# Banks, order of products and the square of a, in a Strassen projection with a gated recurrence

## Chip, cores and metric

The kernel runs on one core of one Trainium2 chip. The metric is the device time of one execution in microseconds. Its engines are named as the profile names them: PE (TensorE) multiplies, DVE (VectorE), ACT (ScalarE) and POOL (GpSimd) work on vectors, SP (SyncE) issues the DMAs. Each works through its own list of instructions in order and waits at the first one whose inputs or target are not free.

## The reference

One layer over 1024 positions of width 2048, all in float32: an RMSNorm, one projection to 6144 columns (queries, keys, values and gate of eight attention heads; input and gate of eight recurrent blocks), the two halves, one output projection, the residual and a last RMSNorm. Cut to what the change touches:

```python
h = rms_norm(x, norm_gain[l])
proj = h @ w_in[l]                       # 1024 x 2048 @ 2048 x 6144
...
r = sigmoid(xb @ w_a + b_a)              # after a causal convolution of width 4
i = sigmoid(xb @ w_x + b_x)
log_a = -8.0 * r * softplus(-lru_lambda)
a = exp(log_a)
mult = sqrt(-expm1(2.0 * log_a))
h[t] = a[t] * h[t - 1] + mult[t] * (i[t] * x[t])
```

The kernel computes `expm1(2 log_a)` as `(a*a + 1) * tanh(log_a)`, so it needs the square of `a`.

## The kernel before

**Products.** The projection is done by blocks of two by two with seven products in place of eight (Strassen, in Winograd's form). A *pair* is two units of 128 output columns over one half of the 2048 inputs; there are 24 pairs for each half of the inputs, 48 in all. For a pair, products 0 to 6 are each twelve matmuls of 128x128 by 128x512 (L677): four blocks of the inputs, and for each the three terms of a float32 split into a high and a low part. A product collects in one PSUM bank; the bank of each is in `BANKS`: al, de, be, al, ga, be, ga for products 0 to 6. Products 3, 5 and 6 add to what the bank holds.

**What reads the banks.** `post` is called behind each product. Behind product 0, ACT copies al (a1, L546). Behind 1, DVE forms result 11 from de and a1. Behind 3, ACT copies al (u2, L552), and DVE forms be + u2 (u3). Behind 4, DVE forms result 22 from ga and u3; behind 5, result 21 from be and u2; behind 6, result 12 from ga and u2. All DVE additions go through the helper `tt`, so they stand at L193 in the profile; the splits into a high part (a cast on ACT, L189) and a low part (DVE or POOL, L190) go through `split`.

**Three segments.** Segment one forms partial results of the eight recurrent pairs over one half of the inputs, segment two all 24 pairs over the other half, segment three the sixteen attention pairs over the first half again. The first two pairs of each segment, and the last two of segments one and two, run side by side in two sets of four banks (pp0 to pp3, and pq0 to pq3). The pairs between them run one behind the other in `chained`, in the banks pp0 to pp3 alone: four pairs in segment one, twenty in segment two, fourteen in segment three. Before the change a link of that chain is 3, 4, 0', 5, 1', 6, 2', where the mark means the next pair.

**Work around it.** What follows a pair is written as generators that a counter of slots drives: one slot passes with every quarter of a product. `recurrent` (segment two) does the convolution, two gates (four groups of three matmuls into pq0 and pq1, sigmoids at L751), the tanh (L760) and the exponential (L762) of the logarithm of a, the square on POOL, (square + 1) x tanh on DVE (L770), its root on ACT (L774), the scan (L781) and the SiLU of the gate (L697, L699), whose product with the scan is made by POOL and split. `rope` and `values` (segment three) rotate q and k and transpose v (on PE, into pq0), and store them by DMA; `square` and `second_operands` (segment one) add up squares of x on ACT and POOL. pq2 and pq3 hold nothing while a chain runs. Weights are loaded and split three products ahead.

A scheduler of the language decides where an instruction stands in the list of its engine, so the lists are not the order of the code; they are fixed when the program is built. 89 buffers of 128x512 are given out in the order in which they come free, so a new use of a buffer can wait for a DMA that still reads the old content.

Of the kernel before, what the change touches and what calls it, by code (L numbers as in the profile page):

```python
# [13 lines left out]
F32 = mybir.dt.float32  # L14
# [3 lines left out]
AF = mybir.ActivationFunctionType  # L18
ALU = mybir.AluOpType
AX = mybir.AxisListType  # L20

P = 128
# [5 lines left out]
NR = 8  # L28
# [25 lines left out]
BANKS = ("al", "de", "be", "al", "ga", "be", "ga")  # L54
# [51 lines left out]
class Pair:  # L106
# [3 lines left out]
    def __init__(self, k, us, done=None, key=None):  # L110
        self.k = k
        self.us = us
        self.done = done
        self.key = key
        self.s = 0
        self.x = {}
        self.w = {}
        self.c = {}
        self.p = {}


class Trunk:
# [86 lines left out]
    def consts2(self):  # L209
# [44 lines left out]
        self.nsp = cst.tile([P, NR], F32, name="nsp")  # L254
        nc.vector.tensor_scalar_mul(self.nsp, t[4], -8.0)


# [280 lines left out]
    def partial(self, pr, name):  # L538
        p = pr.p[name] = self.alloc()
        self.load(p.f, self.part[pr.key, name])  # L540

    def post(self, pr, pi):
        nc, b = self.nc, self.bank[pr.s]
        if pi == 0:
# [20 lines left out]
    def chained(self, pairs):  # L565


        q = [(pairs[0], pi) for pi in range(3)]
        for n, p in enumerate(pairs):
            q += [(p, 3), (p, 4)]  # L570
            for pi in (5, 6):
                if p is not pairs[-1]:
                    q.append((pairs[n + 1], pi - 5))
                q.append((p, pi))
            if p is not pairs[-1]:
                q.append((pairs[n + 1], 2))
        return q

    def projection(self):
# [65 lines left out]
        for i, (p, pi) in enumerate(q):  # L645
# [24 lines left out]
            self.dual = dual  # L670
            acc = self.bank[p.s][BANKS[pi]]
            hi, lo = p.w.pop(pi)
# [30 lines left out]
    def recurrent(self, n, c4):  # L703
# [51 lines left out]
        self.rel(gw)  # L755
        sp = self.nsp[:, n:n + 1]
        th = [self.alloc(), self.alloc()]
# [3 lines left out]
        for l in range(2):  # L761
            nc.scalar.activation(a[l].f, gates[l, 0].f, AF.Exp, scale=sp)  # L762
            self.tt(gates[l, 1].f, gates[l, 1].f, cs[l].f, ALU.mult, nc.gpsimd)
            self.rel(cs[l])
            yield 1
        for l in range(2):
            r = gates[l, 0]
            self.tt(r.f, a[l].f, a[l].f, ALU.mult, nc.gpsimd)
            yield 3
            nc.vector.scalar_tensor_tensor(out=r.f, in0=r.f, scalar=1.0, in1=th[l].f,  # L770
                                           op0=ALU.add, op1=ALU.mult)
            yield 1
# [481 lines left out]
```

## Time and profile before

| | |
|---|---|
| median of 3 runs (range) | 1716.01 us (1712.44 to 1718.68) |
| the profiled execution | 1710.78 us, its span 1709.0 us |
| PE busy, DVE busy | 1561.2 us, 1278.1 us |
| ACT busy, POOL busy | 816.4 us, 615.7 us |
| granted PE clock, mean over the span | 0.972 |
| projection, then attention and output | 0 to 1102 us, 1102 to 1709 us |

The busy time of PE is an average over stages with different limits, and its matmuls overlap; what a stage loses is read from the count of its matmuls against the price of one where nothing waits, and from the waits of PE in that stage.

### The profile page before, as it was taken

Reading aid. Unit: us, or ns where it says so; the run is one execution under the profiler, and the core shown is the slowest. Engines: PE = TensorE matmul, PEld = TensorE weight load, DVE = VectorE, ACT = ScalarE, POOL = GpSimd, SP = SyncE. Lnnn points to the kernel's source line nnn. Section 1 sums busy time; section 2 is a strip of 40 time slices with the busy share of each in tenths; the row PEclk is TensorE's granted clock in tenths of the full one; section 3 lists DMA queues with packets and bytes.
Section 4 is the critical chain, followed back from the end, with each engine's and each line's share of the span. In section 5 each row is a group of like instructions: output and inputs, shape, how many; then the busy total and the mean of one; then the engine's idle time right before and its main releaser. Section 6 shows DMA issues by size and latency. Waiting matters only on the chain. (4 is left out here: it accounts for less than half of the span.)

```text
span 1709.0 us, 22289 instructions
## 1 busy us (share of the span) xinstructions
PE 1561.2 (91%) x7140; PEld 1265.1 (74%) x7140; DVE 1278.1 (75%) x2120; ACT 816.4 (48%) x1462; POOL 615.7 (36%) x486
## 2 busy tenths in 40 slices
PE   6977998998999899998998998889999999989997
PEld 4765876787777777877777777767777777868786
DVE  8856759777987889889999988857777777761412
ACT  6443633645456355653323333335665555663432
POOL 3474421424334234451222222324222322357370
PEclk9998999999999999999999999999999999999999
DMA  6665732433424332575665555877577655474642
GB/s 253 223 219 182 240 119 82 130 95 110 131 79 135 120 120 96 196 237 181 205 198 185 183 181 167 298 287 272 177 228 246 209 164 165 147 249 134 223 153 99
DMA packets 168277, 304.18 MB, mean 178 GB/s; under 512 B 19040, under 2 KB 21216, under 8 KB 168160
## 3 DMA queue, kind: packets, MB, share of 16 engines
q1 hardware_dynamic: 168160, 302.76, 53.3%
q8 instruction: 56, 0.92, 0.2%
q14 instruction: 61, 0.50, 0.1%
HBM read 206.22 MB, written 96.47 MB: 177 GB/s over the span
## 5 line engine op out<-in xcount | busy, mean ns | idle before, releaser
L677 PE MATMUL pp<-b,b 128*128 128x512 f32 x3612 | 881.8, 402 | 96.8 <-ACT b L552 49.5
L677 PEld LDWEIGHTS pp<-b,b 128*128 128x128 f32 x3612 | 696.9, 194 | 263.7 <-ACT b L552 57.5
L190 POOL TENSOR_TENSOR b<-b,b 128x512 fp32r<-128x512 f32 x288 | 429.4, 1504 | 779.8 <-ACT b L189 458.1
L189 ACT CAST b<-b 128x512 fp32r<-128x512 f32 x592 | 353.3, 619 | 526.7 <-DVE b L193 202.1
L190 DVE TENSOR_TENSOR b<-b,b 128x512 fp32r<-128x512 f32 x304 | 234.2, 785 | 74.9 <-ACT b L189 52.5
L193 DVE TENSOR_TENSOR b<-b,b 128x512 f32<-128x512 f32 x340 | 269.7, 809 | 18.0 <-DMA b<-w_in 6.3
L1099 PE MATMUL pq<-b,b 128*128 128x512 f32 x512 | 203.3, 397 | 3.6 <-DVE b L190 3.6
L1098 PE MATMUL pq<-b,b 128*128 128x512 f32 x512 | 203.6, 398 | 1.6 <-POOL b L190 1.6
L1097 PE MATMUL pq<-b,b 128*128 128x512 f32 x512 | 203.0, 397 | 0.0
L193 DVE TENSOR_TENSOR b<-pp,b 128x512 f32<-128x512 f32 x215 | 146.1, 680 | 39.3 <-ACT b L552 22.0
L193 DVE TENSOR_TENSOR b<-pq,b 128x512 f32<-128x512 f32 x89 | 61.0, 686 | 108.4 <-PE pq L1099 102.0
L900 ACT ACTIVATE wide<-sw,mx 128x256 f32<-128x256 f32 (+7 forms) x128 | 93.9, 739 | 61.7 <-DVE mx L896 60.4
L193 POOL TENSOR_TENSOR b<-b,b 128x512 f32<-128x512 f32 (+1 forms) x56 | 82.1, 1469 | 106.1 <-DVE b L699 38.3
L1099 PEld LDWEIGHTS pq<-b,b 128*128 128x128 f32 x512 | 96.7, 189 | 21.4 <-DVE b L190 5.4
L193 DVE TENSOR_TENSOR b<-b,wide 128x512 f32<-128x512 f32 x120 | 104.5, 884 | 9.7 <-ACT wide L1167 9.1
L893 DVE CUSTOM_DVE_ANT_0 sw<-sw,mask 128x256 f32<-128x256 f32 (+7 forms) x128 | 96.7, 762 | 17.9 <-PE sw L889 16.4
L1098 PEld LDWEIGHTS pq<-b,b 128*128 128x128 f32 x512 | 96.8, 189 | 17.5 <-POOL b L190 2.0
L1097 PEld LDWEIGHTS pq<-b,b 128*128 128x128 f32 x512 | 96.8, 189 | 15.9
L677 PE MATMUL pq<-b,b 128*128 128x512 f32 x420 | 104.6, 395 | 2.3 <-POOL b L190 1.0
L677 PEld LDWEIGHTS pq<-b,b 128*128 128x128 f32 x420 | 80.1, 191 | 20.3 <-POOL b L190 1.4
L1024 ACT CAST b<-pq 128x512 fp32r<-128x512 f32 (+1 forms) x80 | 43.5, 544 | 76.7 <-PE pq L1015 73.7
L888 PE MATMUL sw<-b,b 128*128 128x512 f32 (+2 forms) x192 | 70.9, 372 | 9.0 <-ACT wide L900 8.7
(149 smaller groups left out, 1574.6 us busy)
## 6 DMA issues: line engine op xcount, KB each, us to landing
b<-w_in SPq DMA_DIRECT2D x192, 256.0 KB, 2.9
b<-w_out SPq DMA_DIRECT2D x128, 256.0 KB, 4.3
pt<-b SPq DMA_DIRECT2D x96, 256.0 KB, 2.7
b<-pt SPq DMA_DIRECT2D x96, 256.0 KB, 2.9
b<-fs SPq DMA_DIRECT2D x96, 256.0 KB, 4.5
b<-xt SPq DMA_DIRECT2D x72, 256.0 KB, 3.9
fs<-b SPq DMA_DIRECT2D x64, 256.0 KB, 2.4
b<-yd SPq DMA_DIRECT2D x32, 256.0 KB, 4.6
```

The costliest lines, as they stand in the source:

```text
L189: self.nc.scalar.copy(hi.r, x)
L190: (eng or self.nc.vector).tensor_tensor(out=lo.r, in0=x, in1=hi.f, op=ALU.subtract)
L193: (eng or self.nc.vector).tensor_tensor(out=out, in0=a, in1=b, op=op)
L677: nc.tensor.matmul(acc, lhsT=a.r[:, s], rhs=b.r, start=FIRST[pi] and qq == 0 and j == 0, stop=qq == 3 and j == 2, skip_group_check=True)
L888: nc.tensor.matmul(o, lhsT=q[m].r[:, qs], rhs=kk, start=True, stop=False)
L893: nc.vector.tensor_tensor_reduce(out=s, in0=s, in1=self.mask[:, 896 - off:896 - off + cols], scale=1.0, scalar=NEG, op0=ALU.add, op1=ALU.m ...
L900: nc.scalar.activation(p[:, :cols], self.swide[m][:, :cols], AF.Exp, scale=QK ** -0.5, bias=mx[:, m:m + 1], accum_out=sm[:, m:m + 1])
L1024: nc.scalar.copy(wh.r[:, first:], self.tr[:, first:])
L1097: nc.tensor.matmul(acc, lhsT=mh.r[:, s], rhs=wh.r, start=kt == 0, stop=False)
L1098: nc.tensor.matmul(acc, lhsT=mh.r[:, s], rhs=wl.r, start=False, stop=False)
L1099: nc.tensor.matmul(acc, lhsT=ml.r[:, s], rhs=wh.r, start=False, stop=kt == 7)
```

## The change

Three edits. In a chain every second pair (`odd`) has banks of its own for al and be: pq2 and pq3. A link of the chain becomes 3, 4, 0', 1', 5, 6, 2'. And the square of a is no longer a product on POOL but a second exponential on ACT, with twice the scale (`nsp2`), written over the gate; with the product, three slots for each half fall away.

```diff
--- before.py
+++ after.py
@@ -117,6 +117,7 @@
         self.w = {}
         self.c = {}
         self.p = {}
+        self.odd = 0
 
 
 class Trunk:
@@ -253,6 +254,8 @@
         nc.vector.tensor_tensor(out=t[4], in0=t[4], in1=t[3], op=ALU.add)
         self.nsp = cst.tile([P, NR], F32, name="nsp")
         nc.vector.tensor_scalar_mul(self.nsp, t[4], -8.0)
+        self.nsp2 = cst.tile([P, NR], F32, name="nsp2")
+        nc.vector.tensor_scalar_mul(self.nsp2, t[4], -16.0)
 
 
 
@@ -539,8 +542,14 @@
         p = pr.p[name] = self.alloc()
         self.load(p.f, self.part[pr.key, name])
 
+    def banks(self, pr):
+        b = self.bank[pr.s]
+        if pr.odd:
+            b = {**b, "al": self.bank[1]["ga"], "be": self.bank[1]["de"]}
+        return b
+
     def post(self, pr, pi):
-        nc, b = self.nc, self.bank[pr.s]
+        nc, b = self.nc, self.banks(pr)
         if pi == 0:
             pr.a1 = self.alloc()
             nc.scalar.copy(pr.a1.f, b["al"])
@@ -567,13 +576,14 @@
 
         q = [(pairs[0], pi) for pi in range(3)]
         for n, p in enumerate(pairs):
+            p.odd = n % 2
+            nxt = pairs[n + 1] if p is not pairs[-1] else None
             q += [(p, 3), (p, 4)]
-            for pi in (5, 6):
-                if p is not pairs[-1]:
-                    q.append((pairs[n + 1], pi - 5))
-                q.append((p, pi))
-            if p is not pairs[-1]:
-                q.append((pairs[n + 1], 2))
+            if nxt:
+                q += [(nxt, 0), (nxt, 1)]
+            q += [(p, 5), (p, 6)]
+            if nxt:
+                q.append((nxt, 2))
         return q
 
     def projection(self):
@@ -668,7 +678,7 @@
             while dual and not self.dual and self.side:
                 sl.tick()
             self.dual = dual
-            acc = self.bank[p.s][BANKS[pi]]
+            acc = self.banks(p)[BANKS[pi]]
             hi, lo = p.w.pop(pi)
             for qq in range(4):
                 yh, yl = self.Y[OPS[pi]][qq]
@@ -753,20 +763,19 @@
                 yield 2
             self.rel(ch[l], cl[l])
         self.rel(gw)
-        sp = self.nsp[:, n:n + 1]
+        sp, sp2 = self.nsp[:, n:n + 1], self.nsp2[:, n:n + 1]
         th = [self.alloc(), self.alloc()]
         a = [self.alloc(), self.alloc()]
         for l in range(2):
             nc.scalar.activation(th[l].f, gates[l, 0].f, AF.Tanh, scale=sp)
         for l in range(2):
             nc.scalar.activation(a[l].f, gates[l, 0].f, AF.Exp, scale=sp)
+            nc.scalar.activation(gates[l, 0].f, gates[l, 0].f, AF.Exp, scale=sp2)
             self.tt(gates[l, 1].f, gates[l, 1].f, cs[l].f, ALU.mult, nc.gpsimd)
             self.rel(cs[l])
             yield 1
         for l in range(2):
             r = gates[l, 0]
-            self.tt(r.f, a[l].f, a[l].f, ALU.mult, nc.gpsimd)
-            yield 3
             nc.vector.scalar_tensor_tensor(out=r.f, in0=r.f, scalar=1.0, in1=th[l].f,
                                            op0=ALU.add, op1=ALU.mult)
             yield 1
```

New lines: the matmuls stand at L687, the copies of a1 and u2 at L555 and L561, the helpers `tt` and `split` at L194 and L190/L191; in the recurrence, sigmoid, tanh, exponential, second exponential, DVE's step and root stand at L761, L770, L772, L773, L779 and L783.

PE, middle of segment two, from the product 3 of one pair to its product 6, one row (the first of twelve) for each product; before, then after.

```order
L677 MATMUL pp0_78<-b_438_1691,b_846_3529 128x512
...
L677 MATMUL pp2_80<-b_461_1761,b_853_3556 128x512
...
L677 MATMUL pp0_78<-b_382_1500,b_858_3584 128x512
...
L677 MATMUL pp1_79<-b_486_1843,b_862_3608 128x512
...
L677 MATMUL pp3_81<-b_406_1586,b_867_3633 128x512
...
L677 MATMUL pp2_80<-b_506_1907,b_877_3668 128x512
```

```order
L687 MATMUL pq2_68<-b_438_1693,b_849_3538 128x512
...
L687 MATMUL pp2_80<-b_461_1763,b_853_3558 128x512
...
L687 MATMUL pp0_78<-b_382_1502,b_858_3586 128x512
...
L687 MATMUL pp3_81<-b_406_1588,b_862_3610 128x512
...
L687 MATMUL pq3_69<-b_486_1845,b_868_3637 128x512
...
L687 MATMUL pp2_80<-b_506_1909,b_877_3673 128x512
```

Product 0' stands in pp0 both times; product 3 ahead of it was in pp0 too and is now in pq2. Product 1' (pp3) moved ahead of product 5, which is now in pq3.

ACT, the same pair, around the copy of u2 (`b_865`) and the two halves of a recurrence (`b_855`, `b_861` hold its gates); before, then after.

```order
L762 ACT_TABLE_LOAD
L762 ACTIVATE b_871_3642<-b_855_3569,nsp_831 128x512
L751 ACT_TABLE_LOAD
L751 ACTIVATE b_864_3624<-pq0_66,vec_82 128x512
L552 COPY b_865_3629<-pp0_78 128x512
L760 ACTIVATE b_870_3641<-b_861_3606,nsp_831 128x512
L762 ACT_TABLE_LOAD
L762 ACTIVATE b_872_3643<-b_861_3606,nsp_831 128x512
L189 CAST b_877_3668<-b_794_3281 128x512
L189 CAST b_882_3694<-b_844_3524 128x512
L774 ACT_TABLE_LOAD
L774 ACTIVATE b_855_3569<-b_855_3569 128x512
```

```order
L772 ACT_TABLE_LOAD
L772 ACTIVATE b_872_3646<-b_855_3571,nsp_831 128x512
L561 COPY b_865_3631<-pq2_68 128x512
L773 ACTIVATE b_855_3571<-b_855_3571,nsp2_833 128x512
L772 ACTIVATE b_873_3647<-b_861_3608,nsp_831 128x512
L773 ACTIVATE b_861_3608<-b_861_3608,nsp2_833 128x512
L783 ACT_TABLE_LOAD
L783 ACTIVATE b_855_3571<-b_855_3571 128x512
L783 ACTIVATE b_861_3608<-b_861_3608 128x512
L555 COPY b_879_3693<-pp0_78 128x512
```

The two exponentials of a now stand behind one table load, not two, each with a second one (L773), the copy of u2 stands behind the first of them, and the copy of a1 (L546, now L555) behind both roots. Over the whole program ACT has 74 table loads before and 76 after.

SP, segment three, around the stores of v (`vs`), the store of a gate (`gs`), the loads of weights (`w_in`) and of partial results (`pt`); before, then after.

```order
L176 DMA b_1752_7653<-w_in 128x512
L180 DMA vs_1741_7605<-b_1695_7360 128x512
L180 DMA vs_1742_7606<-b_1740_7602 128x512
L176 DMA b_1766_7712<-w_in 128x512
L176 DMA b_1759_7683<-pt_894_3763 128x512
L176 DMA b_1775_7759<-pt_946_4010 128x512
L176 DMA b_1758_7681<-w_in 128x512
L180 DMA vs_1749_7645<-b_1734_7569 128x512
L180 DMA vs_1750_7646<-b_1748_7642 128x512
```

```order
L177 DMA b_1752_7655<-w_in 128x512
L181 DMA vs_1741_7607<-b_1689_7335 128x512
L177 DMA b_1766_7714<-w_in 128x512
L181 DMA vs_1742_7608<-b_1740_7604 128x512
L177 DMA b_1758_7683<-w_in 128x512
L177 DMA b_1759_7685<-pt_895_3768 128x512
L181 DMA gs_1763_7698<-b_1731_7552 128x512
L181 DMA vs_1749_7647<-b_1734_7571 128x512
L181 DMA vs_1750_7648<-b_1748_7644 128x512
```

The load into `b_1758` moved ahead, away from the pair of stores that it stood in front of, and the store of the gate came in there.

## Rows read from the trace of the kernel before

**Rows 1.** The page, part 1: busy us, share of the span, instructions, by engine.
```profile
PE 1561.2 (91%) x7140; PEld 1265.1 (74%) x7140; DVE 1278.1 (75%) x2120; ACT 816.4 (48%) x1462; POOL 615.7 (36%) x486
```

**Rows 2.** Busy us (instructions) by stretch: PE, PEld, DVE, ACT, POOL; clock, DMA share, GB/s.
```profile
80.00:166.00 86.00, 65.78 (x262) 51.96 (x261) 51.87 (x55) 36.71 (x63) 52.81 (x37) 0.90 0.64 205
166.00:244.00 78.00, 78.00 (x344) 64.26 (x343) 53.63 (x76) 36.34 (x64) 29.17 (x19) 1.00 0.56 186
244.00:730.00 486.00, 448.41 (x1896) 364.58 (x1894) 406.02 (x543) 256.16 (x386) 176.21 (x121) 0.96 0.36 117
790.00:1102.00 312.00, 281.93 (x1202) 226.56 (x1201) 289.41 (x412) 108.53 (x188) 79.48 (x48) 0.96 0.62 202
```

**Rows 3.** Waits of PE from 244 to 730 us: total us, times, longest.
```profile
PE pp L677 <- ACT b L552: 31.4, 9, 4.3
PE pp L677 <- ACT b L546: 3.9, 1, 3.9
PE pp L677 <- DVE b L193: 2.0, 1, 2.0
```

**Rows 4.** Timeline, 394 to 403 us: start, us, instruction, idle before it, releaser.
```profile
400.15 1.14 ACT L189 CAST b<-b 128x512 fp32r<-128x512 f32 x2 [5.69 <-POOL b L193]
...
401.20 0.58 ACT L552 COPY b<-pp 128x512 f32<-128x512 f32 x1
...
401.83 1.56 PE L677 MATMUL pp<-b,b 128*128 128x512 f32 x3 [4.16 <-ACT b L552]
...
402.32 0.68 DVE L193 TENSOR_TENSOR b<-pp,b 128x512 f32<-128x512 f32 x1
```

**Rows 5.** Waits of PE from 80 to 166 us.
```profile
PE pp L677 <- DVE b L193: 11.1, 4, 5.4
PE pp L677 <- ACT b L552: 9.1, 2, 6.1
```

**Rows 6.** Waits of PE from 790 to 1102 us.
```profile
PE pp L677 <- DVE b L193: 13.6, 6, 4.4
PE pp L677 <- ACT b L552: 8.9, 6, 2.3
```

**Rows 7.** Busy us of two periods of the middle stretch, columns as in rows 2.
```profile
401.83:515.15 113.32, 104.70 (x444) 85.37 (x445) 92.40 (x124) 59.43 (x90) 42.24 (x29) 0.97 0.35 114
515.15:627.28 112.13, 104.17 (x445) 85.29 (x445) 91.89 (x123) 58.99 (x89) 42.59 (x29) 0.97 0.35 115
```

**Rows 8.** Waits of DVE from 244 to 730 us.
```profile
DVE b L770 <- POOL b L193: 22.5, 6, 7.6
DVE b L190 <- POOL b L193: 12.8, 4, 3.9
```

**Rows 9.** Groups by line: count, busy us, mean ns, idle before and releasers.
```profile
L193 POOL TENSOR_TENSOR b<-b 128x512 f32<-128x512 f32 x16 | 17.0, 1073 | 15.2 <-ACT b L762 8.9 <-ACT b L760 6.2
L762 ACT ACTIVATE b<-b,nsp 128x512 f32<-128x512 f32 x16 | 11.6, 722 | 0.1
L762 ACT ACT_TABLE_LOAD x11 | 14.1, 1283 | 0.2
```

**Rows 10.** Line L770 by itself: count, then shortest, median and longest in ns.
```profile
L770 DVE SCALAR_TENSOR_TENSOR b<-b,b x16: 676/692/1545, 309.2 to 699.5; 128x512 f32<-128x512 f32 x16
```

**Rows 11.** Busy us of a cycle of the third stretch, columns as in rows 2.
```profile
914.38:959.14 44.76, 41.39 (x177) 33.08 (x177) 40.58 (x60) 15.06 (x26) 11.53 (x6) 0.96 0.58 188
```

**Rows 12.** Timeline of a piece of the third stretch, columns as in rows 4.
```profile
889.79 0.59 ACT L189 CAST b<-pq 128x512 fp32r<-128x512 f32 x1 [1.31 <-PE pq L837]
...
892.69 0.33 SPq L176 DMA_DIRECT2D b<-w_in  x1
...
893.07 1.86 SPq L180 DMA_DIRECT2D vs<-b  x2
...
897.01 0.62 ACT L189 CAST b<-b 128x512 fp32r<-128x512 f32 x1 [5.44 <-DMA vs<-b]
...
897.66 0.69 DVE L190 TENSOR_TENSOR b<-b,b 128x512 fp32r<-128x512 f32 x1 [3.62 <-ACT b L189]
```

## The prediction

> **What bounds the kernel now.** The sums of the engines come first: TensorE is busy for 91% of the span and VectorE for 75% [rows 1], so TensorE's time is what can be shortened, and the question is where it waits. The second view is busy time by stretch [rows 2]. The stretch from 166 to 244 us, where pairs run two at a time, shows a product with nothing late: 344 matmuls in 78.00 us, 0.2267 us each, 2.72 us for the twelve of a product. Against that price the first chained stretch (80 to 166) needs 262 x 0.2267 = 59.4 us and takes 86.0; the middle one (244 to 730) needs 1896 x 0.2267 = 429.9 and takes 486.0, so 56.1 us are lost there. In the third (790 to 1102) VectorE is busy 289.4 of 312.0 us. Behind 1102 us the change touches nothing.
>
> The third view is who ended TensorE's waits in the middle stretch [rows 3]: 31.4 us in nine waits, none over 4.3 us, for the copy of u2 (L552); with 3.9 and 2.0 us of others that is 37.3 us. The other 18.8 of the 56.1 us are clock: the granted clock of the stretch is 0.96 [rows 2], and 0.04 x 486 = 19.4.
>
> One of the nine in order of time [rows 4]: ScalarE stands from 394.46 to 400.15 us in front of a cast that waits for a POOL product; the copy of u2 is queued behind it and runs at 401.20; the next pair's product 0 writes the bank that the copy reads, and TensorE has stood still for 4.16 us. VectorE reads the other bank (be + u2) at 402.32 and is done at 403.00. In the first stretch the same two readers cost 9.1 and 11.1 us, in waits of up to 6.1 us [rows 5]; in the third VectorE leads with 13.6 us against 8.9 [rows 6].
>
> **The change part by part: order and banks.** Product 0 of the next pair no longer writes what the copy reads, product 2 no longer writes what result 21 reads, and product 5, which must wait for be + u2, stands three products behind product 4 and no longer two. In [rows 4] TensorE would leave product 4 at 401.83 - 4.16 = 397.67, run products 0 and 1 of the next pair and reach product 5 at 397.67 + 5.44 = 403.11; be + u2 is done at 403.00, and the 4.16 us are gone. Since none of the nine is longer than 4.3 us, I leave 0.2 us to each: 31.4 - 1.8 = 29.6 us. Clock that fell in these waits comes back in proportion: 29.6/37.3 x 18.8 = 14.9 us. That makes 44.5 us, if nothing else becomes late. Products 4 and 6 keep their bank and their distance to its readers, so they gain nothing.
>
> What is late next is VectorE. Two recurrences and five pairs repeat every 112 to 113 us [rows 7]: TensorE needs 444 x 0.2267 = 100.7 us of that and VectorE is busy 92.4. VectorE has waits of its own in it: for the square on POOL (22.5 us in six, three of which, of up to 7.6, hold nearly all) and for another POOL product (12.8 us in four, up to 3.9) [rows 8]. The long ones alternate from one recurrence to the next, so a period holds about 7.6 + 3.9 = 11.5 us, and 92.4 + 11.5 = 103.9 us would be more than TensorE's 100.7.
>
> **The second exponential.** It takes 16 POOL products of 1073 ns away and adds 16 ScalarE instructions of 722 ns, and in the built order the table loads rise from 74 to 76, at 1283 ns [rows 9]: 11.6 + 2.6 = 14.2 us more on ScalarE, which is busy 256 of 486 us. Queued behind them is the copy of u2, which in the piece of order above stands one table load and one exponential behind the sigmoids. What hides this is the 5.44 us of products 0 and 1; without them the two instructions would cost about 2 us in each recurrence. The step L770 on VectorE loses the POOL product and a handover, and be + u2 is now queued ahead of it. No row shows that wait without POOL. Its bounds are 7.6 us (as now) and 0.7 us (one exponential); I take the middle, 3.8 us, which is also the size of the waits in the other recurrences. VectorE's need is then 92.4 + 3.8 + 3.9 = 100.1 us, a tie with TensorE's 100.7. Two chains so close don't overlap fully: I give back 1.5 us in each of 486/112.5 = 4.3 periods, 6.5 us. The middle stretch gains 44.5 - 6.5 = 38 us. With the waits as now it would be 112.5 - 103.9 = 8.6 us a period, less the same 1.5: 31 us; as a lower end I keep 20, half of 38.
>
> L770 takes 692 ns in the median and 1545 at most [rows 10]; the long ones run beside POOL's square. The Trainium skill, "SBUF — State Buffer", "Who interferes with whom", says that a VectorE instruction with two SBUF inputs contends with a GpSimd instruction that reads SBUF, and that ScalarE waits for nobody; the spread of L770 agrees. By that rule alone VectorE would be freed of at most 16 x 0.85 = 13.6 us, some 3 us a period, the tie would be decided for TensorE and the middle stretch would gain 44 us; by the row, the long case is rare (the median is 692), and I keep 38.
>
> **First stretch.** Its waits reach 6.1 and 5.4 us [rows 5], more than or as much as the new cover of 5.44 us, and product 5 still waits for be + u2 there, which comes as late as ScalarE's queue (squares and loads of x) lets it. What is won for sure is nothing; at most product 1, done in the wait, in each of three links: 3 x 2.72 = 8.2 us. I take the middle, 4 us.
>
> **Third stretch.** A cycle of two pairs takes 44.76 us and VectorE is busy 40.58 of it [rows 11]; the rest is one gap. So VectorE is the bound: TensorE's 177 matmuls, eight of them short transposes, need 177 x 0.2267 = 40.1 us at most. The wait for the copy that is taken away moves to product 4 or 5. The gap ends by a chain that doesn't pass TensorE: the load of w_in issued at 892.69 waits for an earlier store to free its buffer, the stores of v stand behind it on SP's queue at 893.07, and ScalarE's cast waits 5.44 us for their landing, VectorE 3.62 us for the cast [rows 12]. In the new order that load takes another buffer and stands ahead; the stores could go out when the cast that fills them, at 889.79, is done (890.4 us), 2.6 us earlier: 6 cycles x 2.6 = 16 us gained. But the gate's tanh now stands ahead of that cast and waits for the landing of the first store of v: some 2 us later, 6 x 2 = 12 us lost. I take 0.
>
> **Sum.** 38 + 4 + 0 = 42 us. The profiled execution took 1710.78 us (a span of 1709.0 and 1.8 around it), 5.2 below the median of 1716.01; 1710.8 - 42 = 1668.8 there, and 1716.0 - 42 = **1674 us** on the scale of the medians.
>
> **Rivals.** (a) VectorE takes over in the middle stretch as well: its waits stay, and half of the gain comes back as waits of product 4. For it: the tie above, and that product 4 keeps its distance; against it: the gaps of VectorE that end on TensorE or a copy shrink by themselves. 20 + 2 - 0 = 22 us: 1694. (b) The third stretch gains too, because the w_in load leaves the stores' way: 42 + 16 = 58 us: 1658. For it the chain in [rows 12]; against it the tanh. (c) Slower. The third stretch has two new waits of ScalarE for stores in every cycle: the tanh for a store of v, a cast for a store of rotated q and k. The nearest row is the cast's 5.44 us; 312/45 = 6.9 cycles with 8 us more are 55 us lost against 42 gained: 1729. It decides from 42/6.9 = 6.1 us a cycle. Against it: ScalarE is busy only 108.5 of 312 us there and mostly waits for VectorE at those places. (d) The banks do nothing: the copy comes so late that product 5 stands where product 0 stood, as in the first stretch: 1714. That would need copies over 5.4 us late, and the nine are at most 4.3. The Trainium skill, "TensorE: Matmul & The Clock Gate", "HAM oscillation — how this bites in real kernels", reports such a case: a second set of PSUM banks brought no further gain in a kernel whose TensorE waited for DMAs. No run here shows that; [rows 3] have no DMA among the waits.
>
> **How the numbers follow.** Forecast 0.50, (a) 0.22, (b) 0.13, (c) 0.09, (d) 0.06. 0.3%, about 5 us, is what a measurement of this kernel can tell from no change. Faster: 0.50 + 0.22 + 0.13 = 0.85; same: (d), 0.06; slower: (c), 0.09. The range leaves (c) and (d) out. Its lower end is the middle stretch without give-back, the first at its best and half of (b): 44.5 + 8.2 + 9 = 62 us, 1654; its upper end the middle at 20, the first at 0 and the third losing 8: 12 us, 1704.
>
> **What would show it.** Right: TensorE's waits for the copy nearly vanish between 244 and 730 us, the period falls to about 103 us, VectorE's waits for POOL at the recurrence fall below 4 us, the third stretch keeps its cycle of 45 us with the waits at product 4 and 5 grown. Wrong: a period over 108 us (a), a cycle of 42 us (b) or of 50 us (c), or new waits of product 5 for VectorE of 4 us each (d).

## The result, and the profile after

The changed kernel takes 1699.17 us in the median of four runs (1693.72 to 1703.45), the kernel before 1714.22 beside it: a ratio of 0.991, 95% interval 0.9889 to 0.9931. That is 15 us faster, where 42 were forecast. The profiled execution took 1698.67 us, its span 1696.9, so 12.1 us less than the span before. Cut at the same pieces of work (first product of a chain to the first of what follows it), the spans say where:

| stretch | before | after | gain | forecast |
|---|---|---|---|---|
| up to the first chain | 61.8 | 60.8 | 1.0 | 0 |
| first chain | 104.4 | 102.8 | 1.6 | 4 |
| pairs side by side | 76.2 | 76.4 | -0.2 | 0 |
| middle chain | 460.1 | 450.6 | 9.5 | 38 |
| pairs side by side | 80.7 | 84.5 | -3.8 | 0 |
| third chain | 318.7 | 314.5 | 4.2 | 0 |
| attention and output | 607.1 | 607.3 | -0.2 | 0 |

Nearly all of what is missing is missing in the middle chain. First its busy times and the third chain's in the kernel before, cut at the same work, then in the kernel after (columns as in [rows 2]):

```profile
242.40:702.50 460.10, 422.62 (x1781) 343.25 (x1780) 378.52 (x510) 239.36 (x358) 166.67 (x116) 0.96 0.34 111
...
783.20:1101.90 318.70, 288.63 (x1233) 232.07 (x1233) 296.11 (x423) 109.59 (x190) 79.38 (x48) 0.96 0.61 200
```

```profile
240.00:690.60 450.60, 417.50 (x1782) 335.20 (x1781) 375.90 (x511) 248.08 (x377) 145.42 (x100) 0.99 0.35 114
...
775.10:1089.60 314.50, 283.57 (x1232) 229.17 (x1231) 294.37 (x422) 108.83 (x189) 72.55 (x48) 0.97 0.64 206
```

The matmuls of the middle chain cost 1780 x 0.2267 = 403.5 us at full price. Above that stood 56.6 us before and stand 47.1 us now. TensorE's waits there after the change (total us, times, longest; they answer to [rows 3]):

```profile
PE pp L687 <- DVE b L194: 12.1, 8, 3.3
PE pq L756 <- ACT b L761: 5.6, 4, 2.1
PE pp L687 <- DVE b L191: 4.5, 6, 1.0
PE pp L687 <- ACT b L555: 3.8, 1, 3.8
PE pq L687 <- DVE b L194: 3.5, 3, 2.1
PE pp L687 <- ACT b L190: 1.6, 3, 0.9
PE pq L687 <- DVE b L191: 1.5, 2, 1.0
```

The 31.4 us for the copy of u2 (L552 before, L561 now) are gone to the last. In their place stand 27 shorter waits: 21.6 us for VectorE (sums at L194, splits at L191), 5.6 of the gates' matmuls for a sigmoid, and 2.0 for ScalarE's casts (a last one of 0.4 us is not among the rows above). The wait for the copy of a1 (L555) was there before, with 3.9 us. In all, 37.5 us of waits have become 33.0. That is 4.5 of the 9.5 us gained. The other 5.0 us came out of what stands above the full price without being a wait: 19.1 us before, 14.1 now. The granted clock rose there from 0.96 to 0.99, which alone would be some 13 us (0.03 x 450); what took the difference wasn't followed.

Where the copy went is in VectorE's own waits, here to the end of the side-by-side pairs (240 to 775.1 us; they answer to [rows 8]):

```profile
DVE b L194 <- ACT b L561: 43.9, 8, 8.5
DVE b L191 <- ACT b L190: 25.0, 11, 6.7
...
DVE b L191 <- POOL b L194: 0.8, 4, 0.2
DVE b L779 <- ACT b L773: 0.5, 1, 0.5
```

VectorE's 22.5 + 12.8 us of waits for POOL are down to 0.8. But its waits for the copy are 43.9 us. Before, over the same work (242.4 to 783.2 us), they were 9.4:

```profile
DVE b L190 <- ACT b L189: 14.2, 10, 2.6
...
DVE b L193 <- ACT b L552: 9.4, 7, 6.4
```

For POOL's products and the copy together nothing is won: 44.7 before, 44.7 now. The waits for ScalarE's casts (L190 now, L189 before) rose as well, from 14.2 to 25.0 us. One of the three longest waits for the copy, in order of time (start, us, instruction, idle before it and its releaser), behind product 3 of recurrent pair 2, which ends at 365.5 us:

```profile
365.73 0.62 ACT L190 CAST b<-b 128x512 fp32r<-128x512 f32 x1 [3.50 <-DMA pt<-b]
366.26 0.68 ACT L761 ACTIVATE b<-pq,vec 128x512 f32<-128x512 f32 x1
...
366.84 0.71 ACT L770 ACTIVATE b<-b,nsp 128x512 f32<-128x512 f32 x1
367.57 1.28 ACT L772 ACT_TABLE_LOAD   x1
...
368.86 0.72 ACT L772 ACTIVATE b<-b,nsp 128x512 f32<-128x512 f32 x1
369.61 1.28 ACT L761 ACT_TABLE_LOAD   x1
370.90 0.69 ACT L761 ACTIVATE b<-pq,vec 128x512 f32<-128x512 f32 x1
371.49 0.58 ACT L561 COPY b<-pq 128x512 f32<-128x512 f32 x1
...
372.10 0.69 DVE L194 TENSOR_TENSOR b<-pq,b 128x512 f32<-128x512 f32 x1 [8.45 <-ACT b L561]
```

A cast, two sigmoids, a tanh, an exponential and two table loads stand between the end of product 3 and the copy on ScalarE, and VectorE, whose list has be + u2 next, stands still for 8.45 us with the splits and sums of other pairs behind it. TensorE itself runs on here; it waits from 379 us on, for a cast and two of VectorE's splits, 1.8 us in three.

The other late copy is that of the attention pair behind it. It is the place of [rows 4], now:

```profile
395.85 0.58 ACT L561 COPY b<-pp 128x512 f32<-128x512 f32 x1
...
396.76 0.68 DVE L194 TENSOR_TENSOR b<-pp,b 128x512 f32<-128x512 f32 x1
...
397.50 3.25 PE L687 MATMUL pp<-b,b 128*128 128x512 f32 x13 [2.08 <-DVE b L194]
```

Product 3 of this pair ended at 387.26 us, so the copy starts 8.59 us behind it, where in [rows 4] it was 6.25. The cover of products 4, 0' and 1' is 3 x 2.72 = 8.16 us; 8.59 + 0.58 + 0.68 and the handovers are over it by the 2.08 us that product 5 waits.

### The profile page after: what moved, and what is told of

Read it like the earlier page. It is cut to its first block, busy times and chain, and to the rows that moved or that the text cites. A ratio compares the mean times of both kernels' runs of the same rounds, so it can differ in the third digit from the quotient of the medians.

```text
span 1696.9 us, 22296 instructions
## 1 busy us (share of the span) xinstructions
PE 1556.5 (92%) x7140; PEld 1257.4 (74%) x7140; DVE 1272.0 (75%) x2121; ACT 825.6 (49%) x1480; POOL 585.7 (35%) x470
## 5 line engine op out<-in xcount | busy, mean ns | idle before, releaser
L687 PE MATMUL pp<-b,b 128*128 128x512 f32 x2700 | 666.6, 401 | 58.2 <-DVE b L194 21.5
L191 POOL TENSOR_TENSOR b<-b,b 128x512 fp32r<-128x512 f32 x288 | 422.2, 1481 | 815.3 <-ACT b L190 459.0
L687 PEld LDWEIGHTS pp<-b,b 128*128 128x128 f32 x2700 | 515.8, 193 | 185.8 <-DVE b L194 28.1
L190 ACT CAST b<-b 128x512 fp32r<-128x512 f32 x592 | 352.5, 620 | 522.2 <-DVE b L194 238.1
L687 PE MATMUL pq<-b,b 128*128 128x512 f32 x1332 | 327.8, 395 | 18.4 <-DVE b L194 13.0
L687 PEld LDWEIGHTS pq<-b,b 128*128 128x128 f32 x1332 | 252.6, 190 | 76.9 <-DVE b L194 16.1
L191 DVE TENSOR_TENSOR b<-b,b 128x512 fp32r<-128x512 f32 x304 | 244.9, 823 | 58.8 <-ACT b L190 46.7
L194 DVE TENSOR_TENSOR b<-b,b 128x512 f32<-128x512 f32 x340 | 267.3, 804 | 21.6 <-DMA b<-w_in 7.5
L1108 PE MATMUL pq<-b,b 128*128 128x512 f32 x512 | 203.5, 398 | 2.8 <-DVE b L191 2.8
L1107 PE MATMUL pq<-b,b 128*128 128x512 f32 x512 | 204.2, 399 | 1.9 <-POOL b L191 1.9
L1106 PE MATMUL pq<-b,b 128*128 128x512 f32 x512 | 203.9, 398 | 0.3 <-ACT b L190 0.3
L194 DVE TENSOR_TENSOR b<-pq,b 128x512 f32<-128x512 f32 x127 | 87.1, 686 | 152.2 <-PE pq L1108 107.9
L194 DVE TENSOR_TENSOR b<-pp,b 128x512 f32<-128x512 f32 x177 | 120.3, 681 | 19.8 <-ACT b L561 17.6
L194 POOL TENSOR_TENSOR b<-b,b 128x512 f32<-128x512 f32 (+1 forms) x56 | 77.8, 1392 | 102.5 <-DVE b L1009 30.3
L1108 PEld LDWEIGHTS pq<-b,b 128*128 128x128 f32 x512 | 96.9, 189 | 20.6 <-DVE b L191 4.2
L1107 PEld LDWEIGHTS pq<-b,b 128*128 128x128 f32 x512 | 97.2, 190 | 17.7 <-POOL b L191 2.2
L1106 PEld LDWEIGHTS pq<-b,b 128*128 128x128 f32 x512 | 97.1, 190 | 16.7 <-ACT b L190 0.8
L194 DVE TENSOR_TENSOR b<-b,wide 128x512 f32<-128x512 f32 x120 | 99.4, 841 | 9.0 <-ACT wide L1176 8.3
```

The costliest lines, as they stand in the source:

```text
L190: self.nc.scalar.copy(hi.r, x)
L191: (eng or self.nc.vector).tensor_tensor(out=lo.r, in0=x, in1=hi.f, op=ALU.subtract)
L194: (eng or self.nc.vector).tensor_tensor(out=out, in0=a, in1=b, op=op)
L687: nc.tensor.matmul(acc, lhsT=a.r[:, s], rhs=b.r, start=FIRST[pi] and qq == 0 and j == 0, stop=qq == 3 and j == 2, skip_group_check=True)
L1106: nc.tensor.matmul(acc, lhsT=mh.r[:, s], rhs=wh.r, start=kt == 0, stop=False)
L1107: nc.tensor.matmul(acc, lhsT=mh.r[:, s], rhs=wl.r, start=False, stop=False)
```

## The experiments

All times are medians; ratios are to the kernel before, run beside each. "Lag" is the time from the end of product 3's last matmul to the start of the copy of u2, worked out from each trace pair by pair; r2 is recurrent pair 2, a21 the attention pair that follows it.

**The parts one by one.** In `bank_order` the square goes back to POOL, with its slots:

```diff
-            nc.scalar.activation(gates[l, 0].f, gates[l, 0].f, AF.Exp, scale=sp2)
...
+            self.tt(r.f, a[l].f, a[l].f, ALU.mult, nc.gpsimd)
+            yield 3
```

> Own banks and the wider order, with the square of a on POOL as before. In the changed kernel TensorE's 31.4 us of waits for the copy of u2 are gone from the middle stretch, but VectorE's waits for that copy rose from 9.4 to 43.9 us, because the copy comes later: behind product 3 of the recurrent pairs by 6.0 us and no longer 1.3. Theory A: the second exponential and the dropped slots push the copy back in ScalarE's list; then here the copy of the recurrent pairs keeps its 1.3 us, VectorE has its waits for POOL again (some 35 us) but not those for the copy (below 20 us), and the time is 1685 to 1697, below the changed kernel's 1699. Theory B: the order of the products itself puts the copy behind the sigmoids, whatever is done with the square; then the copy is 5 to 6 us late here too, VectorE waits for both, and the time is 1703 to 1714.

`exp_only` keeps the exponential, and takes back the banks (no `p.odd`) and the order:

```diff
-            p.odd = n % 2
...
-            if nxt:
-                q += [(nxt, 0), (nxt, 1)]
-            q += [(p, 5), (p, 6)]
+            for pi in (5, 6):
+                if p is not pairs[-1]:
+                    q.append((pairs[n + 1], pi - 5))
+                q.append((p, pi))
...
```

> Only the square of a moved to ScalarE, banks and order as before. Theory A (the exponential pushes the copy of u2 back): TensorE waits longer than 31.4 us for the copy in the middle stretch, since nothing covers it here; some 4 us more for each of eight recurrent pairs, 1725 to 1745. Theory B (the order does it): the copy keeps its place, VectorE's 22.5 us of waits for POOL go, and TensorE, which they don't stop here, gains little: 1706 to 1718.

`order_only` is `bank_order` without `p.odd`, `bank_only` is `bank_order` with the old order:

> Only the wider order; all chained pairs share pp0 to pp3. Product 0 of the next pair still writes the bank that the copy of u2 reads, two products behind product 3, so the copy has its 2.72 us of cover as before and TensorE's waits for it stay at about 31 us: 1708 to 1720 by either theory. If the time falls as it does in the changed kernel (below 1704), the banks are not what brings the gain.

> Only the own banks; the link of the chain is 3, 4, 0', 5, 1', 6, 2' as before. Product 0 of the next pair is free of the copy, and product 5 waits for be + u2 with 5.44 us of cover. With the copies as late as in the kernel before (1.3 and 6.3 us behind product 3, and the addition 0.7 us more) about 2 us of each of the nine waits of 4.3 us stay: 31.4 - 18 = 13 us, and the clock that falls in them with them: a gain of 10 to 25 us, 1690 to 1705. If the copies become later by the banks alone, the time is 1705 or more.

And the two that were not yet together, banks and exponential in the old order:

> Own banks and the second exponential, with the link of the chain as before: 3, 4, 0', 5, 1', 6, 2'. So far: banks alone 0.9907 of the kernel before, exponential alone 0.9973, order alone 1.0005, banks and order together 0.9982, all three 0.991. Theory A: the wider order spoils the place of the copy of u2 in ScalarE's list (5.97 us behind product 3 of the recurrent pairs with banks and order, 1.31 with banks alone); without it the gains of the two others add up: 0.9907 x 0.9973 = 0.988, 1686 to 1693, and the copy of the recurrent pairs stays at 1.3 us. Theory B: banks and exponential work on the same wait and don't add up: 0.990 to 0.993, 1694 to 1701.

Measured, with the lag of two late copies and VectorE's waits in us from the start of the middle chain to that of the third:

| kernel | us | ratio (95%) | lag r2 | lag a21 | for the copy | for POOL's products | both |
|---|---|---|---|---|---|---|---|
| before | 1711 to 1714 | 1 | 1.31 | 6.25 | 9.4 | 22.5 + 12.8 | 44.7 |
| bank_only | 1696.82 | 0.9907 (0.9876 to 0.9937) | 1.31 | 6.29 | 9.2 | 23.5 + 12.7 | 45.4 |
| exp_only | 1706.13 | 0.9973 (0.995 to 0.9996) | 1.31 | 6.63 | 31.4 | 12.7 | 44.1 |
| bank_exp | 1696.82 | 0.9897 (0.9877 to 0.9917) | 1.31 | 6.70 | 33.7 | 12.7 | 46.4 |
| order_only | 1712.73 | 1.0005 (0.9981 to 1.0029) | 1.93 | 5.21 | 46.3 | 0.8 | 47.1 |
| bank_order | 1708.30 | 0.9982 (0.996 to 1.0004) | 6.74 | 9.82 | 45.3 | 0.8 | 46.1 |
| the change | 1699.17 | 0.991 (0.9889 to 0.9931) | 5.97 | 8.59 | 43.9 | 0.8 | 44.7 |

Two of the rows behind the table, VectorE's waits of `bank_only` and of `bank_order`:

```profile
DVE b L780 <- POOL b L194: 23.5, 6, 7.7
DVE b L191 <- POOL b L194: 12.7, 4, 3.9
...
DVE b L194 <- ACT b L561: 9.2, 7, 6.1
```

```profile
DVE b L194 <- ACT b L561: 45.3, 8, 8.5
DVE b L191 <- ACT b L190: 27.6, 10, 6.5
...
DVE b L191 <- POOL b L194: 0.8, 4, 0.2
```

What follows. The times of `order_only`, `bank_only` and `bank_exp` (theory B) came out as expected; theory A of `bank_exp` isn't excluded, since its 0.988 lies in the interval too. `bank_only` missed on the wait: 13 us were expected to stay, and TensorE waits 24.7 us for VectorE. The own banks alone bring as much as the whole change. The wider order alone brings nothing, and on top of the banks it takes their gain away: 0.9907 becomes 0.9982. So of the two theories on `bank_order`, B has the time and the late copy, with the square on POOL as without. But VectorE doesn't wait for both there, as B said: its waits for POOL are 0.8 us. The exponential gains 0.3% alone, nothing measurable on top of the banks, and gives back in the wider order what that lost. `exp_only` also went against what theory A foretold for it (1725 to 1745); TensorE waits 26.2 us for the copy there, not more than 31.4.

Most telling is the last column: whichever parts are in, VectorE stands 44 to 47 us for either the copy or POOL. The name changes, the time doesn't. These waits don't follow the lag: `order_only` has the least lag (52.2 us in the sum of the twenty chained pairs, 64.1 before) and the longest waits. Behind r2, where its copy starts 1.93 us after product 3, VectorE stands 8.82 us for it:

```profile
373.84 0.69 DVE L194 TENSOR_TENSOR b<-pp,b 128x512 f32<-128x512 f32 x1 [8.82 <-ACT b L561]
```

What the order changed is the lists: behind r2 an exponential now stands between the two sigmoids, so that ScalarE makes two table loads ahead of the copy where it made one, and VectorE has be + u2 ahead of the split that waited for POOL's product. The column doesn't set the kernel's time either, since the kernel before and `bank_only` have nearly the same sum and are 1% apart. What the wider order costs on top of the banks shows in TensorE's own waits of the middle chain: 30.0 us in `bank_only`, 38.2 in `bank_order`. Those for VectorE fell from 24.7 to 20.1 us, but those of the gates' matmuls for a sigmoid rose from 0.7 to 9.2 and those for casts from nothing to 4.4. The row of the gates, `bank_only`, then `bank_order`:

```profile
PE pq L756 <- ACT b L761: 0.7, 2, 0.5
```

```profile
PE pq L756 <- ACT b L761: 9.2, 3, 3.2
```

**Who holds VectorE.** First the copy of u2 was given to VectorE:

```diff
-            nc.scalar.copy(pr.u2.f, b["al"])
+            nc.vector.tensor_copy(out=pr.u2.f, in_=b["al"])
```

> The changed kernel with u2 copied by VectorE in place of ScalarE. Theory W: the gain went into VectorE's 43.9 us of waits for ScalarE's copy in the middle stretch. Here these waits are gone and 20 copies of some 0.6 us come to VectorE, 12 us; the period of 110 us falls to 105 or less, some 20 us in the middle; in the third stretch, where VectorE is the bound, 14 copies cost some 8 us: 1682 to 1692. Theory V: VectorE's work with its other waits is the limit, and a wait that goes is replaced by another; then 12 + 8 us more work show in the time: 1700 to 1720.

1695.23 us, ratio 0.9878 (0.985 to 0.9907), between the ranges of the two theories. In the middle theory W fell in this form: the chain takes 452.6 us against 450.6. VectorE's waits for ScalarE's copy are gone, but it now stands 19.4 us for POOL's products (0.8 before) and 13.3 us for TensorE's, beside 3.2 us more work in a period (189.86 us in two, against 183.48). The first chain gained instead, 93.3 us against 102.8.

If all these waits have one source, it is ScalarE's run at the recurrence: sigmoids, tanh, exponentials and the table loads between them. Making both exponentials as tanh gives other values at the same sizes. It leaves out two table loads in each recurrence (60 in the program, 76 in the changed kernel) and no other instruction; but the lists are made anew, and places in them move:

```diff
-            nc.scalar.activation(a[l].f, gates[l, 0].f, AF.Exp, scale=sp)
-            nc.scalar.activation(gates[l, 0].f, gates[l, 0].f, AF.Exp, scale=sp2)
+            nc.scalar.activation(a[l].f, gates[l, 0].f, AF.Tanh, scale=sp)
+            nc.scalar.activation(gates[l, 0].f, gates[l, 0].f, AF.Tanh, scale=sp2)
```

> The changed kernel with the two exponentials of the recurrence made as hyperbolic tangents: other values, the same sizes and places, but no table loads between them and the sigmoids (two of 1.28 us less in each recurrence). In every kernel so far VectorE stands some 8 us in every second recurrence, for POOL's square or for the copy of u2. Theory C (common cause): both come out of the same run of sigmoids, tanhs, table loads and exponentials on ScalarE; 2.6 us less of it bring the copy behind the recurrent pairs from 6.0 to 3.4 us and VectorE's wait of 8.5 to 6 us, the period from 110 to 107 us: 1683 to 1692. Theory V (VectorE stands somewhere else instead): the period stays at 109 to 111 us: 1695 to 1701.

1687.37 us, ratio 0.9853 (0.9817 to 0.9888): theory C. Two periods take 106.3 and 107.3 us, the copy behind r2 comes 4.0 us late. ScalarE's run at the same place, and VectorE's waits to the third chain:

```profile
366.54 0.62 ACT L190 CAST b<-b 128x512 fp32r<-128x512 f32 x1 [3.38 <-DMA pt<-b]
367.06 0.68 ACT L761 ACTIVATE b<-pq,vec 128x512 f32<-128x512 f32 x1
...
369.76 0.71 ACT L770 ACTIVATE b<-b,nsp 128x512 f32<-128x512 f32 x1
370.38 0.57 ACT L561 COPY b<-pq 128x512 f32<-128x512 f32 x1
```

```profile
DVE b L191 <- POOL b L194: 26.7, 4, 6.9
DVE b L191 <- ACT b L190: 18.8, 9, 4.6
...
DVE b L194 <- ACT b L561: 7.0, 4, 4.7
```

From cast to copy ScalarE needs 3.84 us instead of 5.76, though the second tanh now stands ahead of the copy, and copy and POOL together hold VectorE for 33.7 us instead of 44.7. This is the only edit that shortened the sum without touching VectorE's work, so ScalarE's run is a common cause of these waits; that it is the only one isn't shown, since part moved to POOL again.

**No copies.** A pair that finishes a sum of both halves of the inputs needs no copy. VectorE can add the stored half to al at once, then the other bank, in the same number of instructions, and al stays whole since the next pair has another:

```diff
+        if pr.done:
+            self.whole(pr, pi, b)
...
+    def whole(self, pr, pi, b):
+        name, banks = {0: ("11", ("al",)), 1: ("11", ("de",)), 3: ("22", ("al", "be")),
+                       4: ("22", ("ga",)), 5: ("21", ("be", "al")),
+                       6: ("12", ("ga", "al"))}.get(pi, ("", ()))
+        for k in banks:
+            if name in pr.p:
+                pr.c[name] = self.alloc()
+                p = pr.p.pop(name)
+                self.tt(pr.c[name].f, b[k], p.f, ALU.add)
+                self.rel(p)
+            else:
+                self.tt(pr.c[name].f, b[k], pr.c[name].f, ALU.add)
...
-                name = {1: "11", 4: "22", 5: "21", 6: "12"}.get(pi)
+                name = {0: "11", 3: "22", 5: "21", 6: "12"}.get(pi)
```

> The changed kernel; pairs that finish a sum of both halves of the inputs (the recurrent ones in the middle stretch, all in the third) have no copies at all: VectorE adds the stored half to the bank al at once, then the other banks, in as many instructions as before; al stays whole since the next pair has another. ScalarE loses 2 x 0.58 us a pair there. The twelve attention pairs of the middle stretch keep their copies. Theory W (the wait for the copy): the waits of VectorE for the copy fall by those of the recurrent pairs, some half of the 43.9 us, and 10 to 20 us come out: 1678 to 1690. Theory V (VectorE's work is the limit): as much work as before, 1693 to 1702.

> As the run before (no copies for pairs that finish a sum), with the link of the chain as before: 3, 4, 0', 5, 1', 6, 2'. Theory A and W together: the fastest of the four, 1672 to 1686. Theory V: 1690 to 1700.

`after_lean` takes 1653.56 us, ratio 0.965 (0.9629 to 0.9671), 24 us below its range; `bank_exp_lean` takes 1682.93, 0.9815 (0.9791 to 0.9839), within its own, but which of the two is faster is the reverse of what was expected. With the copies gone the wider order, a loss until now, is worth 29 us. In the old order the middle chain gains nothing from the missing copies: 447.5 us, and 448.6 in `bank_exp`. Busy times of the two chains of `after_lean`, then TensorE's waits in its middle chain:

```profile
240.00:665.90 425.90, 410.28 (x1781) 332.59 (x1780) 365.62 (x510) 229.00 (x352) 151.16 (x99) 1.00 0.37 120
752.80:1039.10 286.30, 276.61 (x1233) 226.66 (x1233) 273.42 (x415) 93.72 (x159) 76.06 (x47) 0.99 0.69 222
```

```profile
PE pp L703 <- DVE b L194: 9.0, 8, 2.5
PE pq L772 <- ACT b L777: 4.4, 6, 1.1
PE pq L703 <- DVE b L194: 1.7, 1, 1.7
PE pq L703 <- ACT b L190: 0.4, 1, 0.4
```

The granted clock of the middle is 1.00 and TensorE waits 15.5 us. VectorE's own waits changed their name once more: to the third chain it stands 13.4 us for the copy and 52.8 for ScalarE's casts. ScalarE's list changed too. The sigmoids' table loads in the middle chain, first of the changed kernel, then of `after_lean`:

```profile
L761 ACT ACT_TABLE_LOAD x12 | 15.4, 1283 | 0.2
```

```profile
L777 ACT ACT_TABLE_LOAD x8 | 10.3, 1283 | 0.1
```

With those of the exponentials (12 and 8) and the others the middle chain has 44 loads in the changed kernel and 36 in `after_lean`; `bank_exp` and `bank_exp_lean` have 42 each. So eight loads less, about 10 us of ScalarE, go along with the gain of the middle; what they are worth in it isn't shown. Done for one kind of pair at a time (the condition gets `and pr.k == 1` or `== 0`, and so does the table of names):

> The changed kernel without copies for the recurrent pairs alone (they finish their sums in the middle stretch); the pairs of the third stretch keep copies. Without copies in both, the middle chain (its first product to the two pairs side by side behind it) took 425.9 us against 450.6 of the changed kernel, the third 286.2 against 314.5. Theory W (VectorE's waits for the copy behind the recurrent pairs held the middle): the middle takes 422 to 430 us here, the third 310 to 318: 1670 to 1680 in all. Rival: the middle only gains with fewer buffers in use in the third, or the other way round; then it is 440 or more here.

> The changed kernel without copies for the pairs of the third stretch alone. Theory: VectorE's work bounds the third stretch, and its additions with one operand in PSUM take 683 ns where those of two buffers took 805; the 58 of them that change sides and a shorter queue bring VectorE from 295 to 273 us and the cycle of two pairs from 44 to 40 us: third 284 to 290, middle 446 to 455: 1667 to 1677. Rival: the third gained because the middle left it other buffers and an earlier start; then 305 or more here.

`lean_mid`: 1676.20 us, 0.9793 (0.976 to 0.9827), its middle chain 425.5 us, its third 316.5. `lean_third`: 1678.24, 0.98 (0.9777 to 0.9822), 450.2 and 291.4, just above its ranges. The two gains stand apart and nearly add up. The middle's comes from the recurrent pairs. How much of it is the missing wait, how much VectorE's smaller load (375.9 us before this edit, 365.6 with it) and how much the missing table loads (36 here as well), these runs don't part.

> No copies for pairs that finish a sum, own banks and wider order, but the square of a on POOL as before. Theory: with the copies gone, VectorE's waits for POOL (22.5 and 12.8 us in the middle before) are its longest and stand in front of the sums that TensorE waits for: middle 435 to 445, in all 1663 to 1675. Rival: VectorE has room enough now, and the second exponential is worth nothing: 1650 to 1657.

1649.16 us, 0.9632 (0.9609 to 0.9655): the rival holds, and the second exponential is worth nothing here. With the square on POOL VectorE waits 5.1 us at the recurrence's step, where it was 22.5.

**The fastest.** The copy of u2 by VectorE in the first stretch, where it had helped:

```diff
-            nc.scalar.copy(pr.u2.f, b["al"])
+            if pr.k == 0:
+                nc.vector.tensor_copy(out=pr.u2.f, in_=b["al"])
+            else:
+                nc.scalar.copy(pr.u2.f, b["al"])
```

> As the fastest so far (1653.6; no copies for pairs that finish a sum), with the copy of u2 made by VectorE in the first stretch. With all of these copies on VectorE the first chain had taken 93.3 us against 102.8: 92 to 95 here, 1643 to 1648 in all. If the first chain stays at 101, ScalarE's other work sets it: 1652 to 1656.

> The fastest so far (1645.8) with the square of a on POOL as before. Without copies for the pairs that finish a sum the second exponential gave nothing (0.9632 without it, 0.965 with it): 1641 to 1650. If it is worth something beside VectorE's copies in the first stretch, 1651 or more.

`lean_dve1` takes 1645.83 us, 0.9612 (0.959 to 0.9635), the first chain 93.2 us as expected; with the square on POOL it is 1648.77, 0.9638 (0.9594 to 0.9683), no difference that can be told. `lean_dve1` beats both kernels, by 67 us and by 53.

## Why the prediction was right or wrong

**Right: what bounded TensorE, and what the banks do.** All nine waits for the copy are gone. Where the copy is still late, the cover counts as the prediction counted it (from the end of product 3 it is 8.16 us), against 8.59 and the two instructions behind it.

**Wrong: the step at [rows 4], "be + u2 is done at 403.00, and the 4.16 us are gone".** It took the copy to be as late as before. The lags of the twenty chained pairs add up to 64.1 us before and to 88.9 us after; behind r2 the lag grew from 1.3 to 6.0 us. Own banks alone change it little (71.8 us in sum), the wider order alone shortens it (52.2), and the two together make it long. At this place product 5 still waits 2.08 of the 4.16 us, and new waits for VectorE, the sigmoids and the casts came elsewhere in the period. In the terms of the sum: of 29.6 us of waits 4.5 came out, and of 14.9 us of clock at most 5.0. The 18.8 us that the prediction called clock weren't clock alone, for in `after_lean` 6.6 us above price and waits stay at a granted clock of 1.00 (425.9 - 403.8 - 15.5). The prediction priced order and banks as one edit with one gain. Singly they are a gain of 0.9% and, on top of it, a loss of 0.75%.

**Wrong by its size: the 6.5 us given back.** The sum had VectorE wait 3.8 + 3.9 = 7.7 us in a period, a tie at 100.1 us. Two periods of the changed kernel (columns as in [rows 7]):

```profile
306.95:416.35 109.40, 102.40 (x446) 82.93 (x444) 92.11 (x124) 60.72 (x94) 36.96 (x25) 1.00 0.36 118
416.35:527.48 111.13, 104.08 (x445) 84.08 (x444) 91.37 (x124) 60.75 (x94) 36.47 (x25) 0.98 0.36 117
```

VectorE's work is as forecast, 92.11 and 91.37 us; it stands idle for 17.3 and 19.8 us. The wait for POOL's square did fall below 4 us at each recurrence, as the marker asked, and on top of the banks that was worth nothing that can be measured (`bank_exp` beside `bank_only`). The prediction bounded that wait between 7.6 and 0.7 us by rows on L770 alone, as if POOL were its cause. It is the place where VectorE met ScalarE's run of sigmoids, exponentials and table loads; with POOL taken out, be + u2 meets the same run: in `exp_only`, with order and banks as before, the waits of 7.0 to 7.6 us at L770 are gone, and VectorE stands 8.0 us for the copy at the same recurrences. The prediction even named it, "be + u2 is now queued ahead of it", and put no price there. The rows that could have given one were those of VectorE's waits for the copy: 9.4 us in seven before, up to 6.4. Two slips in the sums change nothing: the middle of 7.6 and 0.7 is 4.15 and not 3.8 us (VectorE's need would be 100.5, still the tie), and half of (b)'s 16 us is 8 and not 9 (a lower end of 1655).

**The rivals.** Case (a) named the mechanism: VectorE takes over in the middle, a period over 108 us (109.4 and 111.1), waits of product 4 and 5 for VectorE. Its price was too small: it left the middle 20 us of gain, and 9.5 were measured. Case (b) didn't come. Of (c), the waits of ScalarE for stores did come in the third stretch: the tanh for stores of v 19.1 us in four, up to 5.6; a cast for stores of rotated q and k 13.4 us in eight. But VectorE waited for that tanh only 7.0 us in nine, 1.2 at most, and a cycle stayed where it was, with VectorE busy for 41.37 of 44.24 us (it answers to [rows 11]):

```profile
945.17:989.41 44.24, 41.36 (x178) 33.30 (x176) 41.37 (x62) 15.58 (x28) 9.21 (x6) 0.96 0.62 200
```

Case (d) is refuted by `bank_only`. The case that the Trainium skill tells in "TensorE: Matmul & The Clock Gate", "HAM oscillation — how this bites in real kernels" (a second set of PSUM banks without further gain, in a kernel rebuilt against its waits for DMAs) isn't this one: the banks are the part that gains most by itself, 0.9907, with no DMA among TensorE's waits.

**First and third stretch.** 1.6 us against 4, and 4.2 against 0: within what was left open. In the first the copy still sits in ScalarE's queue, up to 12.3 us late; only a copy by VectorE shortened that chain (93.3 us), although it too starts up to 12.4 us late. The pairs side by side behind the middle chain cost 3.8 us that the prediction had no term for: they take 82.4 to 88.2 us in every kernel with the second exponential, 79.4 to 80.7 with the square on POOL and 79.7 with tanhs in its place. TensorE waits 5.1 us there where it was 3.4 (one wait of 2.4 us for a cast is the longest), and the granted clock is 0.98 where it was 1.00; what delays the cast wasn't followed. In the third VectorE is the bound as forecast, and TensorE's waits for it went to the transposes of v (13.7 us in six).

## What to carry to other kernels

When a wait is removed, ask who else waits for the same late producer: an engine that works its list in order hands the delay to all that stands behind the waiting instruction, and the profile then shows the same microseconds under another name. Add up a consumer's waits for the releasers in question before and after; if the names change and the sum doesn't move, look further up for what they have in common, and test that by itself. Where a copy out of PSUM only serves to free a bank, look for an order of additions that needs no copy once the bank may live longer. Here the own banks allowed it, and it was worth 46 us with the wider order (1699.17 to 1653.56) and 14 with the old one (1696.82 to 1682.93). And try the parts of a change again after each new one: the wider order was a loss with the copies and a gain without them.

## What the runs showed of the hardware

The third chain of `after_lean` has VectorE busy for 273.4 us, where the changed kernel has 294.4, with nearly as many instructions (415 and 422). One row of each tells a part of it: additions at L194 in the changed kernel's third stretch, by what they read (shortest, median, longest in ns):

```profile
L194 DVE TENSOR_TENSOR b<-b,b x143: 674/687/1832, 775.6 to 1088.5; 128x512 f32<-128x512 f32 x143
...
L194 DVE TENSOR_TENSOR b<-pp,b x56: 676/683/694, 777.5 to 1083.0; 128x512 f32<-128x512 f32 x56
```

Of two buffers in SBUF an addition takes 687 ns in the median and up to 1832; with one operand in PSUM none took over 694. Their means are 805 and 683 ns, so the 58 additions that `after_lean` moves from the first kind to the second save 58 x 0.12 = 7 us. The Trainium skill, "SBUF — State Buffer", "Who interferes with whom", says that a VectorE instruction contends with GpSimd's reads when both of its inputs come from SBUF, and not with one such input; these rows agree. So does the order of time: in the changed kernel's third chain all 20 two-buffer additions of over 800 ns run beside a GpSimd instruction, by more than half a microsecond each, and of those that run beside none, none took over 699 ns. Additions with an operand in PSUM that ran beside one were no longer for it (682 ns in the mean of 17). In `after_lean` only four of the two-buffer additions that are left are over 800 ns, so their mean is 713 ns.
